# A hybrid decoder layer: when the second map's weight sums are loaded and added, and when the next block's inputs begin

## The chip, the cores and the metric

The kernel runs on one core of one Trainium2 chip. The metric is the device time of one execution in microseconds (us).

## The reference

One decoder layer on x of shape (1, 2048, 1024), float32, with a conditioning vector c:

```python
cond = jax.nn.silu(c)
mod = (cond @ w_ada + b_ada)[:, None, :]
sh1, sc1, g1, sh2, sc2, g2 = jnp.split(mod, 6, axis=-1)

h = x * (1.0 + sc1) + sh1
z = h @ w_in                                   # 1024 -> 2048
gate_b, gate_c, v_conv, v_pool = jnp.split(z, [512, 1024, 1536], axis=-1)
y_conv = gate_b * _short_conv(gate_c * v_conv, conv_w)
y_pool = _multiscale_pool(v_pool, w_pool, pool_scale)
mix = jnp.concatenate([y_conv, y_pool], axis=-1) @ w_out
x = _layer_norm(ALPHA * x + (1.0 + g1) * mix, ln1_g, ln1_b)

h = x * (1.0 + sc2) + sh2
f = jnp.square(jax.nn.relu(h @ w_mlp_in)) @ w_mlp_out   # 1024 -> 4096 -> 1024
x = _layer_norm(ALPHA * x + (1.0 + g2) * f, ln2_g, ln2_b)
```

## The kernel before

The 2048 tokens are worked through in two blocks (b) of 1024. Each block passes through the input projection (in_proj_0 or in_proj_1), the output projection (out_proj) and the **first map** (first_map: 1024 -> 4096 with the squared ReLU). The **second map** (down: 4096 -> 1024) then runs once, over both blocks. Every product of float32 matrices is made of three matmuls (mm3, L161 to L164) from a high part (ScalarE, L157) and a low part (VectorE, L158) of each operand; this making of two parts is called a split here.

The large products use schemes with fewer products and more additions. In the first map each of eight groups g (512 columns of the hidden layer) takes seven products instead of eight. The weights of a product come from sums of blocks of w1, made on VectorE as they are needed (block_weights, L585, in block 0) or read back from DRAM (w1sum, in block 1). The activations' seven operands ("11", "21", "22", "1", "2", "3", "4") are made once a block by back, of which "1" to "4" need parts that are read back from DRAM (hsave, L864 and L879). A group's results (c11, c12, c22, c21) are then summed by the list U_SUMS into 26 blocks that the second map reads (usum, stored from the POOL queue, L1080).

The second map takes 26 products over 4 x 4 x 2 blocks (PRODUCTS). Their weights are 8 raw blocks of w2 and 17 sums of them, each made once, in eight column halves g of 512 columns, by **sum_down** (L1145). It follows the list W_SUMS: an entry of two is a load of a block into a register (half of an "o" tile) through SP's queue (L1153), an entry of five an addition on VectorE (all additions have the helper's line, L167), and where its last number is not -1 the result is stored to DRAM (wsum, from the POOL queue, L1159). sum_down is a generator: it hands control back ahead of each addition.

What calls it is **beside**, which up (the first map of one group) calls between its products, four times in group 0 and seven times in each other group. In block 0 beside takes the next step of first_side: four steps that make the gate vector g2 from wada (ada, two loads and two products each), twelve steps of two sum_down entries each, between them four sums of the next block's inputs (sum_x), two of the input projection's weights (sum_weights), and then second_side, which goes on with sum_down, two additions a step. In block 1 beside takes second_side from the start.

At the start of a block, first_map runs the first products of groups 0 and 1 between the steps of back; five calls of beside fall into that part. After the last group of block 0, **prepare** (L698) loads and splits the next block's first weight and three of its seven inputs.

The "o" tiles are a pool of ten buffers of 128 x 1024. A group's four results, its spare tiles for sums, sum_down's two register tiles, the wada rows, sum_x and sum_weights, the parts that back reads from hsave, and out_proj's eight rows of x all come from it. The framework plans the order of each engine's and each queue's instructions when the kernel is built: the earlier in the program, the sooner, but an instruction whose buffer is not free stands back for later ones that can run. On the chip each engine and queue then runs in that order and waits on semaphores.

Of the kernel before, what the change touches and what calls it, by code (L numbers as in the profile page):

```python
# [11 lines left out]
ALU = mybir.AluOpType  # L12
# [6 lines left out]
NB = S // T  # L19
# [5 lines left out]
NC = FF // FC  # L25
# [7 lines left out]
SLOTS = 26  # L33
RAW_SLOT = (0, 4)
U_SUMS = (
# [4 lines left out]
)  # L40
W_SUMS = (
    (3, 6),
    (2, 7),
    (1, 3, 2, -1, 8),
    (0, 4),
    (2, 0, 3, -1, 9),
    (0, 2),
    (3, 0, 3, -1, 10),
    (3, 1, 0, -1, 11),
    (0, 0),  # L50
    (2, 2, 0, 1, 12),
    (2, 1, 0, -1, -1),
    (0, 1),
    (2, 2, 0, 1, 13),
    (2, 3, 0, 1, 14),
    (2, 3),
    (3, 3, 2, 1, 15),
    (3, 5),
    (2, 2, 3, -1, -1),
    (3, 7),  # L60
    (3, 0, 3, -1, 16),
    (3, 2, 3, -1, 17),
    (3, 4),
    (1, 1, 3, -1, 18),
    (0, 1, 0, 1, -1),
    (3, 0, 2, -1, 19),
    (3, 0),
    (0, 0, 3, -1, 20),
    (2, 0, 2, -1, 21),
    (3, 2),  # L70
    (2, 2, 3, 1, 22),
    (2, 5),
    (0, 0, 2, 1, 23),
    (1, 1, 2, 1, 24),
)
W_KEPT = 25
PRODUCTS = (
    (13, 2, 1, True, ((3, 0, 1), (3, 1, 1))),
    (2, 3, 1, True, ((0, 1, 1),)),
    (15, 11, 1, False, ((3, 1, -1),)),  # L80
    (5, 23, -1, False, ((2, 1, -1), (3, 1, 1))),
    (23, 8, 1, False, ((0, 0, 1),)),
    (19, 5, 1, False, ((1, 1, 1),)),
    (25, 4, -1, False, ((1, 0, 1),)),
    (4, 17, 1, True, ((2, 1, -1),)),
    (3, 21, 1, True, ((0, 0, -1), (1, 0, -1), (3, 0, -1))),
    (7, 19, 1, False, ((0, 1, -1),)),
    (0, 12, 1, False, ((1, 0, 1),)),
    (1, 22, -1, False, ((0, 0, -1), (2, 0, -1))),
    (6, 20, 1, False, ((1, 1, 1),)),  # L90
    (21, 7, -1, True, ((1, 1, -1),)),
    (8, 16, 1, False, ((2, 1, -1),)),
    (24, 18, 1, False, ((1, 0, -1),)),
    (10, 14, -1, False, ((2, 0, -1),)),
    (22, 9, 1, False, ((0, 0, -1),)),
    (9, 10, -1, False, ((3, 0, 1),)),
    (20, 24, 1, False, ((0, 1, -1),)),
    (14, 15, -1, False, ((3, 1, 1),)),
    (17, 13, -1, True, ((3, 0, 1),)),
    (11, 3, 1, True, ()),  # L100
    (18, 0, 1, False, ((2, 0, -1),)),
    (16, 1, 1, False, ((2, 1, 1),)),
    (12, 2, -1, True, ((2, 0, 1),)),
)

WARM = (5, 3, 1, 2, 2, 2)
# [13 lines left out]
def tile_hybrid_layer(ctx: ExitStack, tc: tile.TileContext, opening, xT, x, wada, win,  # L120
# [921 lines left out]
    def sum_out(g, tiles):  # L1042
        sum_blocks([gout[i % 2, i // 2 * 2 + g] for i in range(4)], wosum[g], tiles)

    def up(b, g, B, beside):
        X, Y, Z = {}, {}, {}
        order = (0, 1, 5, 4, 6, 7, 3) if g else (0, 1, 7, 4, 5, 6, 3)
        product = seven(summed_weights(w1[g], w1sum[g], order) if b or g < 2 else block_weights(w1[g], w1sum[g]), B)
# [78 lines left out]
        if g == 0:  # L1127
            yield
        else:
            product(5, Z, False)  # L1130
            join(c12, Z)
            beside()
# [11 lines left out]

    def sum_down():  # L1145
        for g in range(NC):
            tiles = [t_o() for _ in range(2)]
            regs = [r[:, hs] for r in tiles for hs in halves]
            for step in W_SUMS:
                if len(step) == 2:  # L1150
                    to, i = step
                    src = w2[i, g // 2] if i < 8 else wsum[i - 8, g // 2]
                    nc.sync.dma_start(regs[to], src[:, halves[g % 2]])  # L1153
                    continue
                yield
                to, x, y, sign, i = step
                tt(regs[to], regs[x], regs[y], ALU.add if sign > 0 else ALU.subtract)
                if i >= 0:
                    nc.gpsimd.dma_start(wsum[i - 8, g // 2][:, halves[g % 2]], regs[to])  # L1159

    def residual():
        ag, ab = row(t_o(D), rows[0]), row(t_o(D), rows[1])
# [10 lines left out]
                yield  # L1173


    def down(g2, close):
        F = close.F
        lo_, hi_ = halves
        banks = {}
# [89 lines left out]
        for k, (n, gp) in enumerate(stream):  # L1269
            if n == last:  # L1270
                break
            if k + 4 < len(stream):
                ready.append(operand(*stream[k + 4]))
            ops = ready.pop(0)
            _, _, _, new, reads = PRODUCTS[n]
            if gp == 0:
                if new:
                    banks[n % 2] = [t_ps() for _ in range(4)]
                if 3 <= n < 12:
                    next(later)  # L1280
# [89 lines left out]
    def first_side():  # L1370
        for n in range(0, 8, 2):
            ada(G2 + n, G2 + n + 2, nc.sync.dma_start, lambda: t_o(D))
            yield
        weights = sums_down
        for n in range(4):
            for _ in range(3):
                next(weights)
                next(weights)
                yield
            sum_x(n)  # L1380
            yield
        g2 = mk(sm, [P, D], F32, "bc", 1)
        row_by_dram(g2, mod[:, G2 : G2 + KD], 1)
        gate.append(g2)
        for p in halves:
            sum_weights(wins[0], winsum, t_o, which=[p])
            yield
        yield from second_side()

    def second_side():  # L1390
        for _ in sums_down:
            next(sums_down, None)
            yield

    gate = []
    sums_down = sum_down()

    def first_map(b, B, back):
        side = second_side() if b else first_side()
        rest = []  # L1400

        def beside():
            next(side, None)

        ups = [up(b, g, B, beside) for g in range(NC)]
        for g in range(2):
            next(ups[g])
            back(1 + g)
        for i in range(3, 7):
            next(ups[0])  # L1410
            back(i)
        for g in range(NC):
            for _ in ups[g]:
                pass

    ready = None
    for b in range(NB):
# [64 lines left out]
```

## Time and profile before

| | |
|---|---|
| median of 3 runs | 1974.24 us (1971.22 to 1982.32) |
| the profiled execution | 1976.97 us, its span 1975.1 us |
| TensorE busy | 1741.5 us, 88% of the span |
| VectorE busy | 1422.5 us, 72% |
| ScalarE busy | 839.7 us, 43% |
| POOL busy (it issues the stores) | 402.2 us, 20% |
| moved by DMA | 481.04 MB, 244 GB/s |
| granted TensorE clock, mean | 0.937 |

A row of the timeline has the start in us from the span's start, the duration in us, engine, source line, operation, what is written and read, how many were merged, and in brackets the idle time before it with what ended that. In a windows table each row is one stretch of the span with its length, then busy time and count for each engine, the granted clock as a share of full speed, the DMA engines' busy share and GB/s. SPq is SP's queue, which issues loads. Tiles are named without their numbers; o<-in_w is a load from a raw weight, in sum_down's case from w2.

### The profile page before, as it was taken

Reading aid. Unit: us, or ns where it says so; the run is one execution under the profiler, and the core shown is the slowest. Engines: PE = TensorE matmul, PEld = TensorE weight load, DVE = VectorE, ACT = ScalarE, POOL = GpSimd, SP = SyncE. Lnnn points to the kernel's source line nnn. Section 1 sums busy time; section 2 is a strip of 40 time slices with the busy share of each in tenths; the row PEclk is TensorE's granted clock in tenths of the full one; section 3 lists DMA queues with packets and bytes.
Section 4 is the critical chain, followed back from the end, with each engine's and each line's share of the span. In section 5 each row is a group of like instructions: output and inputs, shape, how many; then the busy total and the mean of one; then the engine's idle time right before and its main releaser. Section 6 shows DMA issues by size and latency. Waiting matters only on the chain.

```text
span 1975.1 us, 22593 instructions
## 1 busy us (share of the span) xinstructions
PE 1741.5 (88%) x7519; PEld 1422.8 (72%) x7519; DVE 1422.5 (72%) x2222; ACT 839.7 (43%) x1148; POOL 402.2 (20%) x767
## 2 busy tenths in 40 slices
PE   9999986218968875899998889789999999999998
PEld 8888865207756654778886667677788888888887
DVE  7987867327767676688967667667666487686998
ACT  6332463105533335434475433334554434353551
POOL 0223120214444343011010444344200000000000
PEclk9999997659988988999999898989999999999999
DMA  9989684437887778644754778767887688667782
GB/s 390 351 304 354 236 295 132 157 107 243 294 287 244 233 266 278 218 172 175 265 193 138 230 227 272 256 215 243 289 290 255 226 287 319 215 220 245 238 309 75
DMA packets 156357, 481.04 MB, mean 244 GB/s; under 512 B 22728, under 2 KB 23248, under 8 KB 156240
## 3 DMA queue, kind: packets, MB, share of 16 engines
q1 hardware_dynamic: 102112, 306.53, 45.8%
q0 software_dynamic: 54128, 173.07, 24.2%
q8 instruction: 59, 0.97, 0.2%
q14 instruction: 58, 0.48, 0.1%
HBM read 317.50 MB, written 162.01 MB: 243 GB/s over the span
## 4 chain that ended last, share of the span: by engine, by line
PE 41%; issue 11%; DMA 11%; DVE 6%; POOL 3%; ACT 1%; DVEq 0%; SPq 0%; POOLq 0%; ACTq 0%
PE ps L163 14%; PE ps L164 14%; PE ps L162 13%; DVE o L167 4%; DMA o<-in_w 4%; DMA wsum<-o 3%; POOL usum L1080 2%; DMA usum<-o 2%; POOL wsum L1159 1%; DVE w L158 1%; DMA o<-hsave 1%; DVE r L167 0%; DMA xsum<-o 0%; DMA r<-usum 0%; PE ps L841 0%
## 5 line engine op out<-in xcount | busy, mean ns | idle before, releaser
L162 PE MATMUL ps<-h,w 128*128 128x512 f32 x1312 | 530.3, 405 | 145.7 <-ACT h L157 104.1
L164 PE MATMUL ps<-h,w 128*128 128x512 f32 x1312 | 527.4, 403 | 64.9 <-DVE w L158 64.8
L163 PE MATMUL ps<-h,w 128*128 128x512 f32 x1312 | 526.6, 401 | 3.0 <-DVE h L158 2.9
L163 PE MATMUL ps<-h,h 128*128 128x512 f32 (+1 forms) x1064 | 412.4, 388 | 0.9 <-DVE h L158 0.9
L162 PE MATMUL ps<-h,h 128*128 128x512 f32 (+1 forms) x1064 | 412.6, 388 | 0.5 <-ACT h L157 0.5
L164 PE MATMUL ps<-h,h 128*128 128x512 f32 (+1 forms) x1064 | 412.4, 388 | 0.0
L162 PEld LDWEIGHTS ps<-h,w 128*128 128x128 f32 x1312 | 256.9, 196 | 208.2 <-ACT h L157 106.9
L167 DVE TENSOR_TENSOR o<-o,o 128x256 f32<-128x256 f32 (+2 forms) x570 | 272.6, 520 | 153.6 <-DMA o<-in_w 108.0
L164 PEld LDWEIGHTS ps<-h,w 128*128 128x128 f32 x1312 | 255.6, 195 | 128.1 <-DVE w L158 73.9
L163 PEld LDWEIGHTS ps<-h,w 128*128 128x128 f32 x1312 | 256.2, 195 | 60.3 <-DVE h L158 6.3
L1080 POOL DMA_DIRECT2D usum<-o x416 | 222.4, 541 | 237.3 <-DVE o L167 164.7
L157 ACT CAST w<-r 128x1024 fp32r<-128x1024 f32 x156 | 163.5, 1051 | 187.6 <-PE ps L163 174.2
L157 ACT CAST h<-r 128x1024 fp32r<-128x1024 f32 (+1 forms) x140 | 140.7, 1010 | 237.1 <-PE ps L163 109.6
L163 PEld LDWEIGHTS ps<-h,h 128*128 128x128 f32 x1064 | 199.8, 188 | 41.9 <-DVE h L158 1.3
L162 PEld LDWEIGHTS ps<-h,h 128*128 128x128 f32 x1064 | 199.8, 188 | 41.8 <-ACT h L157 0.9
L164 PEld LDWEIGHTS ps<-h,h 128*128 128x128 f32 x1064 | 199.8, 188 | 40.9
L158 DVE TENSOR_TENSOR w<-r,w 128x1024 fp32r<-128x1024 f32 x156 | 189.3, 1220 | 41.1 <-ACT w L157 40.9
L158 DVE TENSOR_TENSOR h<-r,h 128x1024 fp32r<-128x1024 f32 (+1 forms) x140 | 162.6, 1167 | 62.5 <-ACT h L157 62.4
L167 DVE TENSOR_TENSOR o<-o 128x256 f32<-128x256 f32 (+1 forms) x224 | 118.9, 535 | 117.7 <-DMA o<-in_w 52.8
L1159 POOL DMA_DIRECT2D wsum<-o x136 | 73.5, 541 | 347.0 <-DVE o L167 335.7
L1067 ACT ACTIVATE o<-o 128x1024 f32<-128x1024 f32 x48 | 50.9, 1060 | 203.7 <-DVE o L167 203.6
L158 DVE TENSOR_TENSOR h<-w,h 128x1024 fp32r<-128x1024 f32 x104 | 126.7, 1219 | 1.6 <-ACT h L157 1.3
(163 smaller groups left out, 1457.5 us busy)
## 6 DMA issues: line engine op xcount, KB each, us to landing
usum<-o POOLq DMA_DIRECT2D x416, 128.0 KB, 4.5
r<-usum SPq DMA_DIRECT2D x104, 512.0 KB, 5.1
wsum<-o POOLq DMA_DIRECT2D x136, 256.0 KB, 3.5
w<-wsum SPq DMA_DIRECT2D x68, 512.0 KB, 5.3
o<-in_w SPq DMA_DIRECT2D x112, 256.0 KB, 4.1
r<-in_w SPq DMA_DIRECT2D x54, 512.0 KB, 5.2
r<-w1sum SPq DMA_DIRECT2D x40, 512.0 KB, 4.5
w<-in_w SPq DMA_DIRECT2D x36, 512.0 KB, 5.9
```

What stands on the lines that cost most here:

```text
L157: high = nc.scalar.copy(hi, src)
L158: return high.ins, nc.vector.tensor_tensor(lo, src, hi.bitcast(F32), op=ALU.subtract).ins
L162: nc.tensor.matmul(ps, whi, xhi, start=first, stop=False, skip_group_check=goes_on)
L163: nc.tensor.matmul(ps, whi, xlo, start=False, stop=False, skip_group_check=goes_on)
L164: nc.tensor.matmul(ps, wlo, xhi, start=False, stop=last, skip_group_check=goes_on)
L167: return nc.vector.tensor_tensor(out_, a, b_, op=op)
L1067: nc.scalar.activation(r, r, AF.Relu)
L1080: nc.gpsimd.dma_start(usum[slot, g // 2, :, b, g % 2, :], z)
L1159: nc.gpsimd.dma_start(wsum[i - 8, g // 2][:, halves[g % 2]], regs[to])
```

## The change

It has four parts.

1. W_SUMS is rewritten as 11 steps. Each step first makes its additions (two, none in the first step) and then issues the loads of the next one, into registers that no addition of this step touches. sum_down holds three tiles (six registers) where it held two (four), and hands control back once a step. A column half has 12 loads where it had 13, and 20 additions and 17 stores as before.
2. U_SUMS and PRODUCTS are replaced by another form of the same scheme: 33 additions a group as before, two spare tiles where there were three, 26 products as before, of which eight have a negated operand where nine had.
3. beside does nothing until a flag (open_) is set, after the part in which back makes the operands. first_side takes four sum_down steps ahead of each sum_x, and block 1's beside takes sum_down directly. What is left of sum_down at the end is taken by down, one step a unit of work (next(side, None)), where before it was run through ahead of down.
4. prepare is called by turn, from the last group of block 0, ahead of its sixth product, where before it was called after the whole first map.

The diff without the tables U_SUMS and PRODUCTS, and with the old W_SUMS cut:

```diff
 W_SUMS = (
-    (3, 6),
-    (2, 7),
-    (1, 3, 2, -1, 8),
-    (0, 4),
-    (2, 0, 3, -1, 9),
...
+    ((), ((0, 4), (1, 6), (3, 2))),
+    (((2, 0, 1, -1, 8), (4, 3, 1, -1, 9)), ((5, 7),)),
+    (((1, 1, 5, -1, 10), (3, 1, 3, -1, 11)), ((4, 1), (0, 0))),
+    (((5, 4, 5, -1, 12), (2, 2, 0, 1, 13)), ()),
+    (((0, 0, 4, -1, -1), (4, 3, 4, 1, 14)), ((2, 3),)),
+    (((3, 3, 2, 1, 15), (5, 5, 2, -1, -1)), ((4, 5),)),
+    (((5, 5, 4, 1, 16), (2, 1, 0, -1, 17)), ((3, 4),)),
+    (((1, 1, 3, -1, 18), (4, 1, 4, 1, 19)), ()),
+    (((2, 1, 0, -1, 20), (3, 0, 4, -1, 21)), ((5, 3),)),
+    (((4, 4, 5, -1, -1), (0, 0, 4, -1, 22)), ((1, 2), (2, 1))),
+    (((1, 0, 1, -1, 23), (4, 4, 2, 1, 24)), ()),
 )
...
-    def up(b, g, B, beside):
+    def up(b, g, B, beside, turn):
...
         else:
+            if g == NC - 1:
+                turn()
             product(5, Z, False)
             join(c12, Z)
             beside()
...
     def sum_down():
         for g in range(NC):
-            tiles = [t_o() for _ in range(2)]
+            tiles = [t_o() for _ in range(3)]
             regs = [r[:, hs] for r in tiles for hs in halves]
-            for step in W_SUMS:
-                if len(step) == 2:
-                    to, i = step
-                    src = w2[i, g // 2] if i < 8 else wsum[i - 8, g // 2]
-                    nc.sync.dma_start(regs[to], src[:, halves[g % 2]])
-                    continue
+            cs = halves[g % 2]
+            for adds, loads in W_SUMS:
+                for to, x, y, sign, i in adds:
+                    tt(regs[to], regs[x], regs[y], ALU.add if sign > 0 else ALU.subtract)
+                    if i >= 0:
+                        nc.gpsimd.dma_start(wsum[i - 8, g // 2][:, cs], regs[to])
+                for to, i in loads:
+                    nc.sync.dma_start(regs[to], (w2[i, g // 2] if i < 8 else wsum[i - 8, g // 2])[:, cs])
                 yield
-                to, x, y, sign, i = step
-                tt(regs[to], regs[x], regs[y], ALU.add if sign > 0 else ALU.subtract)
-                if i >= 0:
-                    nc.gpsimd.dma_start(wsum[i - 8, g // 2][:, halves[g % 2]], regs[to])
...
-    def down(g2, close):
+    def down(g2, close, side):
...
             if n == last:
                 break
+            next(side, None)
             if k + 4 < len(stream):
...
-        weights = sums_down
         for n in range(4):
-            for _ in range(3):
-                next(weights)
-                next(weights)
+            for _ in range(4):
+                next(sums_down)
                 yield
             sum_x(n)
             yield
...
-        yield from second_side()
-
-    def second_side():
         for _ in sums_down:
-            next(sums_down, None)
             yield
...
     def first_map(b, B, back):
-        side = second_side() if b else first_side()
-        rest = []
+        side = sums_down if b else first_side()
+        open_ = []
 
         def beside():
-            next(side, None)
-
-        ups = [up(b, g, B, beside) for g in range(NC)]
+            if open_:
+                next(side, None)
+
+        def turn():
+            if b + 1 < NB:
+                ready.append(prepare())
+
+        ups = [up(b, g, B, beside, turn) for g in range(NC)]
         for g in range(2):
             next(ups[g])
             back(1 + g)
         for i in range(3, 7):
             next(ups[0])
             back(i)
+        open_.append(True)
         for g in range(NC):
             for _ in ups[g]:
                 pass
 
-    ready = None
+    ready = []
     for b in range(NB):
-        B, back = out_proj(b, in_proj_1(*ready) if b else in_proj_0())
+        B, back = out_proj(b, in_proj_1(*ready[0]) if b else in_proj_0())
         first_map(b, B, back)
-        if b == 0:
-            ready = prepare()
-    for _ in sums_down:
-        pass
-    close = Close()
-    down(gate[0], close)
+    down(gate[0], Close(), sums_down)
```

More of the change, by code (lines that the diff above doesn't have):

```diff
@@ L35 @@
 U_SUMS = (
[4 rows of a table removed]
[4 rows of a table added]
 )
 W_SUMS = (
-    (3, 6),
-    (2, 7),
-    (1, 3, 2, -1, 8),
-    (0, 4),
-    (2, 0, 3, -1, 9),
[L47 to L74, printed above, removed]
[11 rows of a table added]
 )
@@ L77 @@
 PRODUCTS = (
[L78 to L103, printed above, removed]
+    (11, 2, 1, True, ((3, 0, 1), (3, 1, 1))),
+    (1, 3, 1, True, ((0, 1, 1),)),
+    (17, 11, 1, False, ((3, 1, -1),)),
+    (5, 21, 1, False, ((2, 1, -1), (3, 1, 1))),
+    (24, 10, 1, False, ((0, 0, 1),)),
+    (21, 5, 1, False, ((1, 1, 1),)),
+    (23, 4, -1, False, ((1, 0, 1),)),
+    (4, 16, -1, True, ((2, 1, -1),)),
+    (3, 22, 1, True, ((0, 0, 1), (1, 0, 1), (3, 0, 1))),
+    (6, 24, 1, False, ((0, 1, -1),)),
+    (0, 13, -1, False, ((1, 0, -1),)),
+    (2, 23, 1, False, ((0, 0, -1), (2, 0, -1))),
+    (8, 20, -1, False, ((1, 1, -1),)),
+    (20, 7, -1, True, ((1, 1, -1),)),
+    (9, 12, -1, False, ((2, 1, 1),)),
+    (25, 18, 1, False, ((1, 0, -1),)),
+    (12, 14, 1, False, ((2, 0, 1),)),
+    (22, 8, 1, False, ((0, 0, -1),)),
+    (7, 9, 1, False, ((3, 0, -1),)),
+    (19, 19, 1, False, ((0, 1, -1),)),
+    (13, 15, 1, False, ((3, 1, -1),)),
+    (15, 17, -1, True, ((3, 0, 1),)),
+    (18, 3, 1, True, ()),
+    (14, 0, 1, False, ((2, 0, -1),)),
+    (10, 1, 1, False, ((2, 1, 1),)),
+    (16, 2, -1, True, ((2, 0, 1),)),
 )
```

8 rows, old and new, of the table U_SUMS are left out of this document.

## The prediction

> **What bounds the kernel now.** I read the page's parts 1 and 2 first, then TensorE's stages, then its longest idle times, and last the queues that stood in the way.
>
> ```profile
> span 1975.1 us, 22593 instructions
> PE 1741.5 (88%) x7519; PEld 1422.8 (72%) x7519; DVE 1422.5 (72%) x2222; ACT 839.7 (43%) x1148; POOL 402.2 (20%) x767
> PE   9999986218968875899998889789999999999998
> PEclk9999997659988988999999898989999999999999
> ```
>
> TensorE is the bound nearly everywhere. Counting slices from 0, it falls away in 6 to 15 (block 0's first map) and a little in 21 to 26 (block 1's), and there the granted clock falls too. The stages, in one table by windows: block 0's first map up to the first matmul after its long stall, the rest of that map, block 1's two projections, block 1's first map in the same two parts, and the second map.
>
> ```profile
> core 0: us, PE busy (x) PEld busy (x) DVE busy (x) ACT busy (x) POOL busy (x), PEclk, DMA share, GB/s
> 275.30:438.90 163.60, 60.80 (x249) 48.27 (x247) 73.29 (x110) 35.81 (x45) 23.06 (x43) 0.67 0.45 154
> 438.90:795.00 356.10, 281.90 (x1134) 223.92 (x1135) 254.56 (x450) 151.04 (x182) 151.38 (x283) 0.89 0.78 261
> 795.00:1040.40 245.40, 242.59 (x1084) 199.95 (x1084) 194.40 (x271) 121.39 (x194) 25.67 (x45) 0.99 0.58 205
> 1040.40:1112.00 71.60, 58.76 (x231) 46.07 (x232) 46.97 (x63) 32.78 (x39) 11.89 (x23) 0.88 0.46 146
> 1112.00:1410.00 298.00, 267.80 (x1121) 217.02 (x1121) 201.24 (x387) 124.89 (x148) 124.66 (x233) 0.94 0.75 243
> 1410.00:1975.10 565.10, 556.24 (x2475) 460.99 (x2473) 419.39 (x523) 252.58 (x348) 10.14 (x19) 1.00 0.71 248
> ```
>
> The last row gives the price of a matmul when nothing is in its way: 556.24 / 2475 = 0.2247 us. At that price the second row's 1134 matmuls need 254.8 us of its 356.1, so 101 us are lost there, idle and slow clock together; the fifth row's 1121 need 251.9 of 298.0, so 46 are lost. Rows one and four are the same program part in the two blocks (transposes, the making of seven operands, the first products), yet one takes 163.6 us and the other 71.6.
>
> TensorE's longest idle times, from its timeline (the bracket is the idle time before the instruction, and what ended it):
>
> ```profile
> 289.01 0.48 PE L841 MATMUL ps<-ident,o 128*128 128x128 f32 x1 [6.49 <-DVE o L167]
> 329.79 0.79 PE L162 MATMUL ps<-h,w 128*128 128x512 f32 x1 [14.95 <-ACT h L157]
> 438.93 0.79 PE L162 MATMUL ps<-h,w 128*128 128x512 f32 x1 [78.85 <-ACT h L157]
> 794.72 0.79 PE L164 MATMUL ps<-h,w 128*128 128x512 f32 x1 [17.75 <-DVE w L158]
> ```
>
> The 78.85 us is a hole in which VectorE adds weights and the other engines stand. Its cause is read from SP's, ScalarE's and VectorE's timelines in turn:
>
> ```profile
> 357.54 4.62 SPq L1153 DMA_DIRECT2D o<-in_w  x3
> 367.29 61.46 SPq L1153 DMA_DIRECT2D o<-in_w  x10
> 432.37 5.09 SPq L879 DMA_DIRECT2D o<-hsave  x2
> 437.83 1.04 ACT L157 CAST h<-o 128x1024 fp32r<-128x1024 f32 x1 [76.90 <-DVE o L167]
> 412.40 0.69 DVE L167 TENSOR_TENSOR o<-o,o 128x512 f32<-128x512 f32 x1 [5.31 <-DMA o<-in_w]
> 436.57 1.23 DVE L167 TENSOR_TENSOR o<-o,o 128x1024 f32<-128x1024 f32 x1 [4.23 <-DMA o<-hsave]
> ```
>
> Operand "4" needs the two hsave loads (L879), and these stand on SP behind 13 loads of L1153: exactly one full set of W_SUMS. Each add of 0.69 us waits up to some 5 us for a load that could not be issued until the register was free. I infer why the set stands first: hsave needs two of the ten "o" buffers, and two of those were held by sum_down until its set was through.
>
> Outside the hole the same adds hold VectorE up all through both first maps (its waits, first 438.9 to 795, then 1112 to 1410, last the w2 loads of the whole profile; columns: sum in us, times, longest):
>
> ```profile
> DVE o L167 <- DMA o<-in_w: 49.9, 23, 4.8
> DVE o L167 <- DMA wsum<-o: 12.0, 4, 6.4
> ...
> DVE o L167 <- DMA o<-in_w: 55.6, 25, 5.4
> DVE o L167 <- DMA wsum<-o: 17.5, 11, 4.6
> ...
> DVE o L167 <- DMA o<-in_w: 160.8, 65, 5.4
> ```
>
> That is 61.9 us in the one and 73.1 in the other, on an engine that runs in order, so the weight splits and the additions out of PSUM queue behind.
>
> **The change part by part.** The sum is made against the profiled execution's 1976.97 us, 2.7 above the median of the three runs shown.
>
> *No sums before the operands exist (open_).* Five calls of beside per block now do nothing. In the order of the changed kernel's instructions the L879 hsave loads stand on SP ahead of all wada loads and all w2 loads, and their adds on VectorE ahead of the first wada product. So the hole's cause is gone. What is late next is what the fourth row shows, where no sum stood in the way before either: 71.6 us for 231 instructions. With 249 it is 71.6 + 18 x 0.2247 = 75.6, against 163.6: 88 us gained. The eight wada products that filled this part move into the next one:
>
> ```profile
> 284.64 1.23 DVE L278 SCALAR_TENSOR_TENSOR o<-o,o 128x1024 f32<-128x1024 f32 x1 [4.95 <-DMA o<-in_wada]
> L1153 SPq DMA_DIRECT2D o<-in_w x44: 327/328/762, 492.0 to 788.6; - x44
> DMA to landing us min/median/max: 2.6/4.5/8.7
> L1159 POOL DMA_DIRECT2D wsum<-o x136 | 73.5, 541 | 347.0 <-DVE o L167 335.7
> ```
>
> They are 8 x 1.23 = 9.8 us of VectorE. There it is busy 254.56 of 356.1 us, so between 0 and 9.8 show; I take 4. Net 84.
>
> *Two additions a step, loads a step ahead, three tiles instead of two.* Per column half 12 loads instead of 13 (eight fewer in all, 0.33 us each on SP: 2.6 us, hidden, as SP mostly waits); the 20 additions (0.69) and 17 stores (0.54 on POOL) stay. A step now ends with the loads for the next, so a load has one product of 24 matmuls, 24 x 0.2247 = 5.4 us, to land. The landing row (of L1153, 438.9 to 795) has a median of 4.5 and a longest of 8.7, so most waits vanish and some stay. Leaving out the 17.75 us gap, which is the next part's, 101.3 - 17.8 = 83.5 us were lost. Bounds: nothing comes back, if the split waits have other causes; or all of it. I take six tenths, 50 us, nearer the upper end because 61.9 us of VectorE's waits are these loads and stores. In block 1 the additions run on, in the changed order, to the last two groups, which had none. There the bounds are -10 and 46; I take 20.
>
> *Next block's inputs begin sooner (turn).* prepare is moved ahead of the last group's products 5 and 6 and of the sums after them on VectorE; its loads now stand among the last w2 loads on SP, and it has none on POOL. Before, ScalarE and VectorE made the first weight so:
>
> ```profile
> 773.80 1.04 ACT L157 CAST w<-r 128x1024 fp32r<-128x1024 f32 x1 [1.56 <-DMA r<-in_wins]
> 793.45 1.22 DVE L158 TENSOR_TENSOR w<-r,w 128x1024 fp32r<-128x1024 f32 x1
> ```
>
> The second half of that split came 19 us after the first, behind the last group's sums, and cost TensorE the 17.75 us. In the changed order it stands ahead of product 5's own weight split, with five adds of the weights (0.69) and two input subtractions (1.22) between them. So the gap goes, and product 5 may wait instead: 5 x 0.69 + 2 x 1.22 = 5.9 us, of which I let 4 show. Bounds 0 and 17.75; I take 14.
>
> *Other tables.* 33 additions a group in U_SUMS before and after, with two spare tiles where there were three; four fewer negated operands, whose instructions cost what the plain ones do. The second map has no loss to give: zero. The sums that end in it are the last two additions, 1.4 us, under a VectorE 419 of 565 us busy; if that cover failed, 1.4 us.
>
> Sum: 84 + 50 + 20 + 14 = 168. 1976.97 - 168 = 1809, less 2.7 for the median: 1806 us.
>
> **The rivals.**
>
> *All of the stalls go.* If VectorE's load waits are the cause of nearly everything lost, 84 + 75 + 40 + 16 = 215 come back: 1759. For it: 61.9 and 73.1 us of waits against 83 and 46 lost. Against it: VectorE stays 72% busy there and so has its own work to wait for. 18%.
>
> *The clock comes back whole.* After a long gap the matmuls are slow for a while: the one at 331.70, 1.9 us behind the gap of 14.95, took 0.63 us, and the line's mean is 403 ns.
>
> ```profile
> 331.70 0.63 PE L164 MATMUL ps<-h,w 128*128 128x512 f32 x1
> L164 PE MATMUL ps<-h,w 128*128 128x512 f32 x1312 | 527.4, 403 | 64.9 <-DVE w L158 64.8
> ```
>
> The clock's share of what is lost is 281.90 - 254.8 = 27 us in the second stage and 267.80 - 251.9 = 16 in the fifth. My sum takes six and four tenths of it back, 23. If gaps that are only shortened leave the clock alone, all 43 come back: 20 more, 1786. The Trainium skill (TensorE: Matmul & The Clock Gate, "Part 1: The HAM clock gate") says that the clock halves only after an idle window of about 3.4 us and recovers after as much work. The gap of 14.95 agrees; no row above shows a short gap by itself. 8%.
>
> *The DMA engines become the bound.* The second stage has 0.78 of 356.1 us, 278 us of transfer, which does not shrink with the gaps. Loads issued early then land late. If half of the 50 and nothing of block 1's 20 come back, 84 + 25 + 0 + 5 = 114: 1860. The Trainium skill (DMA: Bandwidth & Descriptors, "Issuing engines are not separate DMA queues") says that all queues share the same 16 engines; the stage table cannot tell that from a slow queue. 15%.
>
> *The change doesn't do what it says: the hole comes back in another place,* where a set of sums again holds "o" buffers that the path needs. Then 50 + 20 + 14 remain and the 84 don't: 1890. Against it: in the changed order each set of the first map ends before out_proj, which takes eight of ten. 4%.
>
> *Slower: three register tiles starve the pool of ten.* Six for a group's results and sums and three for sum_down leave one. The next group's second result then waits for a store to land.
>
> ```profile
> ACT o L1055 <- DMA usum<-o: 15.3, 3, 8.2
> ```
>
> It has happened three times, 8.2 at the longest. If it hit both results of each of 14 later groups at that length, 14 x 2 x 8.2 = 230 us would go, against 168 gained: 2036. It decides from 168 / 28 = 6 us each. Against it: 4 + 3 + 2 buffers before are as many as 4 + 2 + 3. 4%.
>
> **How the numbers follow.** The forecast keeps 50%. The range 1740 to 1870 takes in the first three rivals, with a little beyond the first since the bounds (88, 83.5, 46, 17.75) add up to 235, which is 1739. Half a percent, 10 us, is about what a measurement tells from no change (the three runs lie 11 apart). Faster by that: the forecast and the first four rivals, 0.95; within it 0.01, left for a gain that other waits eat up; slower 0.04.
>
> **What would show it.** Right: no TensorE gap over 20 us; the hsave loads of L879 ahead of every w2 load; the first map's first part near 76 us in both blocks; VectorE's waits on w2 loads below 50 us in the whole profile, from 160; the second map still 565. Wrong: a stretch of ten w2 loads in a row with TensorE idle, or a DMA share over 0.9 with VectorE still waiting for loads.

## The result and the profile after

The changed kernel takes 1848.5 us (median of 4 runs, 1846.85 to 1848.79) against 1975.22 (1971.22 to 1982.32) for the kernel before, run beside it: a ratio of 0.9353, 95% interval 0.9325 to 0.9381. That is 127 us faster, inside the predicted range, and 42 us short of the predicted 1806. Its profiled execution took 1848.79 us, its span 1846.8.

The page's parts 1 and 2 of the changed kernel:

```profile
span 1846.8 us, 22581 instructions
PE 1726.5 (93%) x7519; PEld 1415.0 (77%) x7519; DVE 1420.4 (77%) x2222; ACT 840.1 (45%) x1148; POOL 402.7 (22%) x767
PE   9999998777959889999988999899999999999998
PEclk9999998888989999999989999999999999999999
```

The work is the same (7519 matmuls, 2222 VectorE instructions). TensorE's dips in slices 6 to 15 have become shallower (5 tenths at the lowest, in slice 11, where slice 8 had 1), and the clock no longer falls below 8 tenths. The same six stages by windows, cut at the same matmuls as before (columns as in the prediction):

```profile
275.00:347.20 72.20, 57.90 (x248) 45.91 (x247) 49.90 (x70) 35.41 (x45) 13.90 (x26) 0.92 0.50 168
347.20:682.50 335.30, 275.57 (x1134) 221.65 (x1135) 260.31 (x462) 150.49 (x181) 147.88 (x277) 0.89 0.85 291
682.50:930.20 247.70, 242.45 (x1085) 200.28 (x1083) 197.31 (x279) 123.18 (x196) 29.48 (x52) 0.99 0.57 202
930.20:1000.30 70.10, 57.50 (x232) 45.22 (x233) 46.88 (x63) 32.49 (x39) 11.83 (x23) 0.90 0.44 143
1000.30:1281.70 281.40, 263.36 (x1121) 213.87 (x1120) 213.46 (x407) 124.48 (x148) 133.98 (x250) 0.98 0.86 281
1281.70:1846.80 565.10, 556.14 (x2474) 461.16 (x2472) 419.42 (x523) 252.80 (x348) 10.29 (x20) 1.00 0.70 249
```

Stage by stage, before minus after: 163.6 - 72.2 = 91.4 (predicted 88); 356.1 - 335.3 = 20.8 (predicted 50 - 4 + 14 = 60); 245.4 - 247.7 = -2.3; 71.6 - 70.1 = 1.5; 298.0 - 281.4 = 16.6 (predicted 20); 0. The sum is 128, and nearly the whole miss lies in the rest of block 0's first map. (The time is nearer to the 1860 of the rival with the DMA engines than to 1806; the runs below tell whether that rival was at work.)

SP's queue after (timeline), where the hole was: the hsave loads for operand "4" (L857 now) stand ahead of the wada and w2 loads.

```profile
340.15 3.08 SPq L857 DMA_DIRECT2D o<-hsave  x2
343.33 0.88 SPq L566 DMA_DIRECT2D r<-in_w  x2
349.46 25.49 SPq L265 DMA_DIRECT2D o<-in_wada  x8
375.05 1.33 SPq L1136 DMA_DIRECT2D o<-in_w  x3
```

What is left in the rest of block 0: its three largest TensorE gaps, the ScalarE instructions that stood ahead of the casts behind the first and the third (timelines of TensorE and of ScalarE), then VectorE's waits, in the whole profile and (last two rows) in this stage:

```profile
387.44 0.79 PE L140 MATMUL ps<-h,w 128*128 128x512 f32 x1 [9.57 <-ACT w L135]
452.88 0.80 PE L142 MATMUL ps<-h,w 128*128 128x512 f32 x1 [10.04 <-DVE w L136]
552.77 0.79 PE L140 MATMUL ps<-h,w 128*128 128x512 f32 x1 [18.65 <-ACT w L135]
```

```profile
384.28 1.08 ACT L1118 ACTIVATE o<-ps 128x512 f32<-128x512 f32 x2 [8.78 <-DMA usum<-o]
539.24 1.08 ACT L1118 ACTIVATE o<-ps 128x512 f32<-128x512 f32 x2 [12.30 <-DMA winsum<-o]
```

```profile
DVE o L145 <- DMA o<-in_w: 62.5, 34, 6.2
DVE o L145 <- DMA wsum<-o: 9.7, 4, 6.3
...
DVE o L145 <- DMA o<-in_w: 25.0, 9, 6.2
DVE o L145 <- DMA wsum<-o: 3.4, 3, 1.6
```

VectorE's waits on w2 loads fell from 160.8 us to 62.5 (the prediction's sign was below 50), in this stage with the stores from 61.9 to 28.4. ScalarE stands at c21 (L1118) for an "o" buffer whose store has not landed, with the weight casts queued behind it. This is not new: the kernel before waited 11.1 us for a store of winsum at the same place. Behind the third gap ScalarE has two more waits, 3.00 us for a store of usum and 4.16 us for an addition on VectorE, before the cast.

### The profile page after: what moved, and what is told of

The parts are those of the page before. It is cut to its first block, busy times and chain, and to the rows that moved or that the text cites. A ratio compares the mean times of both kernels' runs of the same rounds, so it can differ in the third digit from the quotient of the medians.

```text
span 1846.8 us, 22581 instructions
## 1 busy us (share of the span) xinstructions
PE 1726.5 (93%) x7519; PEld 1415.0 (77%) x7519; DVE 1420.4 (77%) x2222; ACT 840.1 (45%) x1148; POOL 402.7 (22%) x767
## 5 line engine op out<-in xcount | busy, mean ns | idle before, releaser
L140 PE MATMUL ps<-h,w 128*128 128x512 f32 x1312 | 523.9, 400 | 58.8 <-ACT w L135 34.5
L142 PE MATMUL ps<-h,w 128*128 128x512 f32 x1312 | 522.7, 399 | 38.2 <-DVE w L136 38.2
L141 PE MATMUL ps<-h,w 128*128 128x512 f32 x1312 | 521.9, 398 | 8.1 <-DVE h L136 8.0
L140 PEld LDWEIGHTS ps<-h,w 128*128 128x128 f32 x1312 | 252.5, 193 | 118.5 <-ACT w L135 37.3
L142 PEld LDWEIGHTS ps<-h,w 128*128 128x128 f32 x1312 | 253.1, 193 | 97.6 <-DVE w L136 44.6
L145 DVE TENSOR_TENSOR o<-o,o 128x256 f32<-128x256 f32 (+2 forms) x554 | 266.0, 524 | 70.5 <-DMA o<-in_w 23.9
L141 PEld LDWEIGHTS ps<-h,w 128*128 128x128 f32 x1312 | 253.1, 193 | 64.3 <-DVE h L136 11.1
L135 ACT CAST h<-r 128x1024 fp32r<-128x1024 f32 (+1 forms) x144 | 144.8, 1011 | 240.4 <-PE ps L141 131.1
L136 DVE TENSOR_TENSOR h<-r,h 128x1024 fp32r<-128x1024 f32 (+1 forms) x144 | 167.5, 1170 | 86.0 <-ACT h L135 85.8
L145 DVE TENSOR_TENSOR o<-o 128x256 f32<-128x256 f32 (+1 forms) x240 | 124.9, 528 | 69.2 <-DMA o<-in_w 38.6
L145 DVE TENSOR_TENSOR o<-o,ps 128x512 f32<-128x512 f32 x172 | 114.1, 683 | 22.9 <-PE ps L142 19.5
```

Source lines behind the costliest of these rows:

```text
L135: high = nc.scalar.copy(hi, src)
L136: return high.ins, nc.vector.tensor_tensor(lo, src, hi.bitcast(F32), op=ALU.subtract).ins
L140: nc.tensor.matmul(ps, whi, xhi, start=first, stop=False, skip_group_check=goes_on)
L141: nc.tensor.matmul(ps, whi, xlo, start=False, stop=False, skip_group_check=goes_on)
L142: nc.tensor.matmul(ps, wlo, xhi, start=False, stop=last, skip_group_check=goes_on)
L145: return nc.vector.tensor_tensor(out_, a, b_, op=op)
```

## The experiments

Line numbers differ from kernel to kernel. The stages are cut at the same matmuls in all, and come from one profiled execution of each. The ratio compares a kernel with the kernel before of its own group of runs (medians 1970.63 to 1978.89 us). Differences in us in the text are those of the times, where no ratio is named; by the ratios they would be up to 6 us larger or smaller.

| kernel | us | ratio to before, 95% | block 0 first part | its rest | block 1 rest |
|---|---|---|---|---|---|
| before | 1975.22 | 1 | 163.6 | 356.1 | 298.0 |
| changed | 1848.5 | 0.9353 (0.9325 to 0.9381) | 72.2 | 335.3 | 281.4 |
| no_flag | 1874.56 | 0.9485 (0.9458 to 0.9513) | 97.1 | 330.0 | 271.3 |
| no_lead | 1851.5 | 0.9376 (0.9357 to 0.9396) | 72.4 | 345.5 | 279.9 |
| prep_after | 1851.58 | 0.9372 (0.9354 to 0.939) | 71.7 | 341.1 | 277.8 |
| sums_late | 1890.48 | 0.9576 (0.9551 to 0.96) | 72.0 | 287.5 | 368.2 |
| no_adds | 1805.38 | 0.9157 (0.9137 to 0.9177) | 72.4 | 321.8 | 254.5 |
| two_tiles | 1918.49 | 0.9737 (0.971 to 0.9764) | 70.9 | 375.8 | 315.5 |
| two_tiles_no_flag | 1927.72 | 0.9775 (0.975 to 0.9801) | 94.5 | 359.4 | 309.8 |
| pool_adds | 1900.55 | 0.9642 (0.9612 to 0.9673) | 72.3 | 365.9 | 304.0 |
| w5 | 1888.38 | 0.9541 (0.951 to 0.9571) | 80.3 | 353.7 | 298.2 |
| w5_o11 | 1870.42 | 0.9454 (0.9428 to 0.948) | 71.7 | 346.4 | 299.8 |
| gate_late | 1873.76 | 0.9465 (0.9432 to 0.9497) | 71.8 | 343.4 | 288.1 |
| before_new_u | 1906.52 | 0.9672 (0.9652 to 0.9692) | 96.3 | 366.4 | 288.8 |

**no_flag.**

```diff
-        open_ = []
+        open_ = [True]
```

> The changed kernel (1848.5 us) with beside working from the start of each block again (open_ set at once). The first map's first part in block 0 took 163.6 us before and 72.2 after. Theory of the prediction: the hole came from sums taken before the operands exist, so without the flag it comes back: first part over 130 us, total over 1900 us. Rival: the flag is only half of it. In this kernel's order only four w2 loads stand on SP ahead of the hsave loads of operand 4, where a full set of 13 stood before, because three tiles and loads a step ahead let a set go on differently. Then the first part takes some 72 + 8 x 1.23 (the wada products are back in it) + a few load waits = 85 to 95 us, the rest of block 0's map gets shorter by about as much, and the total lies within 10 us of 1848.5.

The first part grew by 25 us, not by 91, and block 1's by as much. Both stages by windows:

```profile
275.20:372.30 97.10, 59.32 (x248) 46.92 (x246) 60.75 (x91) 35.77 (x45) 14.99 (x28) 0.80 0.59 197
945.80:1041.00 95.20, 60.14 (x232) 46.98 (x233) 59.98 (x83) 32.87 (x39) 21.02 (x40) 0.78 0.56 184
```

Against 72.2 and 70.1 with the flag. The rests got 5 and 10 us shorter, and the total 26 longer. The rival came nearer for block 0's first part, the total lies between the two. So the flag is worth about 26 us, and most of the hole is gone without it. In block 1 it keeps out a loss that the kernel before did not have. There the first part took 71.6 us without any flag, and 71.0 in two_tiles_no_flag (below); with three tiles and loads a step ahead, SP's queue has ten w2 loads ahead of block 1's first hsave loads:

```profile
945.81 11.39 SPq L1136 DMA_DIRECT2D o<-in_w  x4
...
960.58 0.33 SPq L1136 DMA_DIRECT2D o<-in_w  x1
...
968.04 1.62 SPq L1136 DMA_DIRECT2D o<-in_w  x2
...
975.91 5.34 SPq L1136 DMA_DIRECT2D o<-in_w  x3
986.37 1.27 SPq L842 DMA_DIRECT2D o<-hsave  x2
```

**no_lead.** Each step's loads go ahead of its own additions.

```diff
+            due = ()
             for adds, loads in W_SUMS:
+                for to, i in due:
+                    nc.sync.dma_start(regs[to], ...)
+                due = loads
...
-                for to, i in loads:
-                    nc.sync.dma_start(regs[to], ...)
```

> The changed kernel with each step's loads issued ahead of its own additions instead of at the end of the step before; tables, three tiles, additions, stores and flag as they are. It prices the lead alone, for which the prediction took 50 us in block 0 and 20 in block 1 (with the change of form). Theory A (VectorE's waits for w2 loads are what the lead takes away, and they reach TensorE): the waits on w2 loads go from 62.5 us back to 130 to 160, and the total grows by 35 to 70 us, about 1885 to 1920. Theory B (the lead takes VectorE's waits away, but most of them were off the path; block 0's rest is held by the other work of first_side): the waits grow just as much, but the total by under 20 us.

3 us, within the intervals of no change. The waits on w2 loads hardly moved (62.5 in the changed kernel); those on the stores of sums grew from 9.7 to 22.1 us:

```profile
DVE o L145 <- DMA o<-in_w: 61.0, 30, 8.0
DVE o L145 <- DMA wsum<-o: 22.1, 9, 5.4
```

Neither theory held, since both expected the waits on w2 loads to double. Block 0's rest grew by 10.2 us, and the projections behind it and block 1 gave most of that back. The framework's plan seems to put a load where its register comes free, wherever the program has it, so that the lead lies in the free registers (the next two runs).

**prep_after.** The call of turn stands after the whole first map.

```diff
-            if g == NC - 1:
-                turn()
             product(5, Z, False)
...
+        turn()
```

> The changed kernel with prepare called after the whole first map of block 0 again, as before. It prices the earlier inputs alone. Theory of the prediction: the gap of 17.75 us before the projections of block 1 comes back, and 14 us net are lost: 1862.5 us. Rival 1: the gap was the tail of the sums of the last group, which now run otherwise, so under 5 us are lost: below 1853.5. Rival 2: earlier inputs cost as much on the last group as they save (ties within 3 us).

3.1 us longer, within the intervals; not the predicted 14. The gap of 17.75 us did not come back as one. TensorE's timeline has two in its place:

```profile
680.98 0.80 PE L140 MATMUL ps<-h,w 128*128 128x512 f32 x1 [7.03 <-ACT w L135]
...
687.49 0.79 PE L142 MATMUL ps<-h,w 128*128 128x512 f32 x1 [4.44 <-DVE w L136]
```

Block 0's rest grew by 5.8 us, and the other stages gave part of it back. Rival 1 held; rival 2, a tie within 3 us, can't be told from it.

**two_tiles and two_tiles_no_flag.** sum_down in its old form (its code as before), with a list of 32 entries for four registers, worked out for the new sums; the second also sets the flag at once. These show what the lead lives on, and whether the hole comes back.

```diff
-            tiles = [t_o() for _ in range(3)]
+            tiles = [t_o() for _ in range(2)]
...
```

> The changed kernel with sum_down as before in form: two tiles (four registers), each load directly ahead of the addition that needs it, two additions a call; same sums, again 20 additions, 12 loads (one of them of a stored sum). The flag and the tables of the first map stay. Moving the loads alone had cost 3 us. Theory R (what lets a load run ahead is a free register, so the third tile is the lead): VectorE's waits on w2 loads go from 62.5 us to over 120, block 0's rest from 335 to 350 or more, block 1's from 281 to 295 or more, total 1875 to 1910 us. Rival P (the ten buffers are what is short in block 0; one buffer more free for results and for first_side is worth as much as the lead): the total stays within 10 us of 1848.5 or falls, with the longest waits of ScalarE on stores (12.3 us) gone.

> The kernel two_tiles with beside working from the start of each block again. With three tiles and no flag the first part of block 0's first map took 97.1 us where it took 163.6 before and 72.2 with the flag. Theory of the prediction (two register tiles, held until the set is through, keep the hsave loads back): the hole comes back in this kernel, first part over 140 us, total 45 us or more over two_tiles. Rival S (the third spare tile of the old first map's sums was what left no buffer for hsave; with two spares there is room): the first part is 85 to 105 us, as with three tiles, and the total within 30 us of two_tiles. In this kernel's order three w2 loads stand ahead of the first hsave load of operand 4 and one more ahead of the second, which speaks for S.

VectorE's waits in the whole of two_tiles:

```profile
DVE o L166 <- DMA o<-in_w: 132.1, 55, 7.1
DVE o L166 <- DMA wsum<-o: 22.5, 11, 5.9
```

Theory R held in its direction: without the third tile the waits double, and 70 us are lost, 40.5 in block 0's rest and 34.1 in block 1's; the total passed its upper end. The 70 us are an upper bound for the tile, since the order of this list is my own: two_tiles_no_flag is 21 us slower than before_new_u (below), which keeps the old list. With two tiles the flag is worth 9 us (1927.72 - 1918.49), with three 26. Without the flag the first part took 94.5 us. So two register tiles and a missing flag together do not bring the hole of 163.6 back, and rival S's times held.

**before_new_u.** The kernel before, with the changed kernel's U_SUMS and nothing else. Its second map still reads the stored blocks by the old numbers, so it computes something else; the work is the same.

```diff
 U_SUMS = (
-    ((1, 5, -1, 1, 16), (0, 1, 1, 2, 1), (16, 0, 1, 3, 19)),
+    ((0, 1, 1, 1, 16), (1, 5, -1, 2, 1), (17, 0, 1, 3, 19)),
...
```

> The kernel before with one thing changed: its list U_SUMS is that of the changed kernel (33 additions a group, two spare tiles instead of three). The list W_SUMS and PRODUCTS stay, so the numbers of the second map are others; the work is the same. Two register tiles, no flag, loads just ahead of their additions, prepare after the first map. Theory S (the hole stood there because the third spare tile left no buffer for the hsave loads until a whole set of sums was through): three w2 loads, not 13, stand on SP ahead of the hsave loads of operand 4 here, so the first part of block 0's first map takes 90 to 105 us instead of 163.6. The set that ran in the hole then costs its price in the rest (10 calls at about 1.3 us), so the total is 45 to 65 us below 1974, 1909 to 1929 us. Theory of the prediction (sums taken too early by two register tiles held until the set ends; the flag was needed): the hole stays, first part over 140 us, the total within 15 us of 1974.

Its first part and the rest of block 0 by windows, then SP's queue:

```profile
275.10:371.40 96.30, 59.29 (x249) 46.94 (x247) 60.95 (x93) 35.74 (x45) 15.04 (x28) 0.80 0.58 196
371.40:737.80 366.40, 282.74 (x1135) 225.15 (x1136) 267.12 (x468) 152.49 (x184) 160.13 (x298) 0.87 0.81 275
```

```profile
351.42 9.12 SPq L1153 DMA_DIRECT2D o<-in_w  x3
362.04 0.33 SPq L879 DMA_DIRECT2D o<-hsave  x1
...
371.22 0.33 SPq L879 DMA_DIRECT2D o<-hsave  x1
```

Three w2 loads ahead of the first hsave load, where 13 stood before: the list alone takes 67 us out of the first part and gives 10 back in the rest; in block 1's rest it brings 9.2. In all it brings 65 us, half of the change's 127. It was the edit that the prediction costed at zero. The old list takes its third spare tile in its second row, which group 0 runs just ahead of operand "4", and the new one never takes a third. That this tile is what matters was not separated from the order of the additions: no run changed the one without the other. Nor does the old list make a hole wherever it runs: in block 1 of the kernel before, with no flag either, the hsave loads stood ahead of the w2 loads (71.6 us). And no run has the old list with the flag, so whether the flag alone would have removed the hole stays open.

**sums_late and no_adds.** The first takes no step of sum_down in block 0 and two a call in block 1; the second leaves the 160 additions out, stores loaded blocks in place of sums, and keeps loads, stores and tiles.

```diff
-                next(sums_down)
                 yield
...
+    def second_side():
         for _ in sums_down:
+            next(sums_down, None)
             yield
...
-        side = sums_down if b else first_side()
+        side = second_side() if b else first_side()
```

```diff
-                    tt(regs[to], regs[x], regs[y], ALU.add if sign > 0 else ALU.subtract)
                     if i >= 0:
-                        nc.gpsimd.dma_start(wsum[i - 8, g // 2][:, cs], regs[to])
+                        nc.gpsimd.dma_start(wsum[i - 8, g // 2][:, cs], regs[got])
                 for to, i in loads:
+                    got = to
...
```

> The changed kernel with no step of sum_down in block 0; block 1's beside takes two steps a call instead. It tells what holds the rest of block 0's first map, which took 335.3 us with 1134 matmuls (254.8 us at 0.2247 each, so 80.5 us are lost). Theory B (the waits behind ada, sum_x and the sums of the projection's weights, whose loads are used at once and whose tiles come from the same ten buffers): with sum_down's loads, additions and three tiles all gone, at least half of the loss stays: the stage over 295 us. Theory A (sum_down's own loads and additions hold it): the stage falls to 255 to 275 us. Block 1's rest, 281.4 us with 48 steps, takes 88: longer by 10 us if the lead covers the loads, by 40 or more if they come late at a DMA share that would pass 0.95.

> The changed kernel without sum_down's 160 additions: loads (256 KB each), stores, the three tiles and the steps stay, what is stored is a loaded block (so the second map's weights are others). Without any of sum_down, block 0's rest had fallen from 335.3 to 287.5 us; this tells which part of it did that. Theory V (VectorE runs in order; an addition that waits for its load, 25.0 us there, and the 0.69 us of each hold up the weight splits): the stage falls to 285 to 305 us and block 1's rest from 281.4 to 258 to 268; the total to 1775 to 1810 us. Rival D (DMA engines busy 0.85 of the stage, and buffers that stay held until stores land): the stage stays over 320 us, block 1's over 275, and the total over 1825 us.

The two rests by windows, first of sums_late, then of no_adds:

```profile
347.50:635.00 287.50, 266.24 (x1135) 217.07 (x1135) 223.38 (x399) 153.64 (x185) 118.71 (x222) 0.95 0.76 253
951.80:1320.00 368.20, 280.18 (x1121) 223.56 (x1120) 258.78 (x479) 121.96 (x145) 168.82 (x315) 0.87 0.87 294
```

```profile
347.60:669.40 321.80, 276.26 (x1135) 222.16 (x1136) 225.35 (x404) 152.42 (x184) 153.17 (x286) 0.91 0.91 318
983.20:1237.70 254.50, 254.15 (x1121) 210.12 (x1120) 167.10 (x327) 125.93 (x148) 134.37 (x250) 1.00 0.95 312
```

The two blocks differ. In **block 1** the additions with their waits are nearly the whole loss: without them 254.5 us, below theory V's range, where 1121 matmuls at full speed need 251.9. There the DMA engines are busy 0.95 of the stage at 312 GB/s, and TensorE loses 2.6 us: rival D, as it was put, is out there. The run takes away an addition's own time (80 x 0.69 = 55 us in this stage) and its wait for a load (36.5 us in the changed kernel) together, so it can't say whether loads that landed late were behind the loss. In **block 0** rival D's bound was met (321.8, over 320). Taken away in this order, the loss of 80.5 us (335.3 - 254.8) falls into 13.5 us that go with the additions (335.3 - 321.8), 34.3 that go with sum_down's loads, stores and tiles (321.8 - 287.5), and 32.7 that stay with no sum_down at all. For sums_late both thresholds were missed, 287.5 lying between them; the 40 steps put into block 1 cost it 86.8 us, 2.2 each, where the 38 taken from block 0 had cost 1.3.

**pool_adds.**

```diff
-                    tt(regs[to], regs[x], regs[y], ALU.add if sign > 0 else ALU.subtract)
+                    nc.gpsimd.tensor_tensor(regs[to], regs[x], regs[y], op=...)
```

> The changed kernel with sum_down's 160 additions on POOL instead of VectorE, nothing else changed. No row shows what POOL takes for one; VectorE takes 0.69 us, POOL is busy 22% of the span. Theory V (VectorE's order is what the additions disturb): block 0's rest falls to 290 to 315 us, block 1's to 260 to 270, total 1790 to 1825 us. Rival (POOL also issues the stores of the first map's sums, which then queue behind additions that wait for loads, so buffers come free later; or the two engines slow each other): the stage stays at 335 us or grows, total 1850 to 1930 us, and ScalarE's and VectorE's waits on usum stores grow.

The rival's times held, 52 us slower. POOL's additions from the groups, then the weight splits on VectorE, in pool_adds and in the changed kernel (duration in ns min/median/max):

```profile
L1132 POOL TENSOR_TENSOR o<-o,o 128x512 f32<-128x512 f32 x96 | 145.4, 1517 | 19.1 <-DMA o<-in_w 13.1 <-DMA wsum<-o 4.3
L136 DVE TENSOR_TENSOR w<-r,w x156: 1205/1221/5743, 47.6 to 1295.0; 128x1024 fp32r<-128x1024 f32 x156
```

```profile
L136 DVE TENSOR_TENSOR w<-r,w x156: 1205/1221/1232, 47.1 to 1256.7; 128x1024 fp32r<-128x1024 f32 x156
```

POOL takes 1.52 us where VectorE takes 0.69, and a split of VectorE took up to 5.74 us (at 503.45, across three additions on POOL), where none takes over 1.23 without POOL's additions. The Trainium skill (SBUF — State Buffer, "Who interferes with whom") says that a VectorE instruction with two SBUF inputs contends with a GpSimd instruction that reads SBUF; the trace agrees, 5.74 against 1.23 us. Of the rival's two reasons only this one is seen: ScalarE's and VectorE's waits on usum stores did not grow (22.6 us in the changed kernel, 22.1 here).

**w5, w5_o11 and gate_late.** An eleventh "o" buffer, paid with a sixth w buffer, and its control; and the gate vector's wada work moved to block 1 (its lines go from first_side into a second_side that block 1 takes).

```diff
-        return mk(big, [P, w], dt, "o", 10)
+        return mk(big, [P, w], dt, "o", 11)
...
-        return mk(big, [P, T], dt, "w", 6)
+        return mk(big, [P, T], dt, "w", 5)
```

> The changed kernel with five w buffers instead of six: the control for the kernel w5_o11, which needs that space. Weights are split into pairs of w buffers, so five give two pairs and one more half. Both theories expect it to be slower than 1848.5, by 5 to 40 us; only its difference to w5_o11 tells something.

> The control w5 with eleven o buffers instead of ten. Theory P (in block 0's rest the ten buffers are what is short: there ScalarE waited 12.3 us for a store of the projection's weights and 8.8, 4.9 and 3.0 us for stores of the first map's sums before it could write an o tile, 29 us in all, and TensorE's gaps of 9.6 and 18.7 us stand behind the first two): block 0's rest is 12 to 30 us shorter than the control's, those waits fall below 12 us, and the total is 10 to 35 us below the control. Rival L (loads that come late and VectorE's order hold the stage, a buffer more only lets SP load sooner): less than 6 us.

> The changed kernel with the four ada steps of the gate vector g2 (eight wada tiles from the ten buffers, eight products of 1.23 us) at the start of block 1's beside calls instead of block 0's; the sums of the second map then begin four calls sooner in block 0. Theory P: the gap of 9.6 us at 387 us, where the ada tiles held buffers, goes, and nothing as large comes in block 1, whose calls have no sum_x and no sums of the projection's weights beside them: total 5 to 15 us less, 1833 to 1843 us. Rival: the work costs in block 1 what it cost in block 0, or sums of the second map fill the place at 1.3 us a step: within 4 us of 1848.5.

The rest of block 0 in w5 and in w5_o11:

```profile
355.40:709.10 353.70, 283.23 (x1136) 224.31 (x1134) 262.42 (x467) 153.60 (x184) 150.44 (x281) 0.90 0.83 277
```

```profile
346.80:693.20 346.40, 282.36 (x1135) 223.62 (x1134) 263.20 (x469) 153.39 (x184) 149.94 (x280) 0.91 0.83 281
```

The buffer is worth 7.3 us there, between the theories' bounds, and 18 in all, 8.6 of it in the first part. ScalarE's waits for stores fell in this stage from 31.3 us to 15.3, its longest, on the store of winsum, only from 12.5 to 11.2. gate_late missed in sign: 25 us slower (22 by the ratio), with 8.1 us more in the rest of block 0 though the wada tiles were gone from it, and 12.2 more in block 1's two parts. The gap of 9.57 us at 387 did not go but moved: one of 11.99 stands at 401.83, again behind a wait of ScalarE for a usum store. Four more steps of sum_down took the wada work's place in block 0, so the run shows that moving this work gains nothing, not that its tiles cost nothing. No kernel here with the layer's whole work beats the changed one.

## Why the prediction was right, and where it was wrong

- **The hole (88 us; 91.4 measured).** The size held, and so did the sign that was named: hsave loads ahead of every w2 load, 72.2 and 70.1 us in the two blocks. The reason given did not. "So the hole's cause is gone" was credited to open_; the form of U_SUMS, under *Other tables* at zero, takes 67 out by itself, and behind it the flag is worth 25 us there. The step that failed is the inference that "two of those were held by sum_down until its set was through", as the whole reason: with two tiles and no flag, but the new list, the hole stays away. That the flag would have done it with the old list, no run shows.
- **The shares.** Three kernels make a chain from before to changed: before_new_u (0.9672), no_flag (0.9485), changed (0.9353). In this order U_SUMS brings 65 us, the new W_SUMS with its third tile, PRODUCTS and the earlier inputs 37, and the flag 26. The prediction gave them 0, 84 (50 + 20 + 14) and 84. Another order could share it out otherwise, since the flag and U_SUMS act on the same hole. But that the total came near with such shares is in part luck.
- **Two additions a step, three tiles, in block 0 (50 us).** This is the mis-sized term. The stage gave 20.8, where 60 were forecast with the other two terms; the predicted 4 for the wada work is near the 5.3 us by which no_flag's rest is shorter. The step was "because 61.9 us of VectorE's waits are these loads and stores". Those waits did fall, to 28.4 (25.0 and 3.4), though the loads landed later than in the row that the prediction used (median 5.0 us and longest 10.3, where it had 4.5 and 8.7). But without any additions only 13.5 of the stage's 80.5 us come back. A wait on VectorE counts by what stands behind it, and in this stage TensorE mostly waited for something else too. What the remaining 34.3 and 32.7 us are stays open between late loads and buffers held by stores: one buffer more gave 7.3, and moving the wada work gave none.
- **The same in block 1 (20 us; 16.6, and 1.5 in the first part).** Here the step held as to the loss: no_adds shows that VectorE's additions and their waits make it. The gain is less its own: before_new_u, with two tiles and the old W_SUMS, already has 288.8 us, so 9.2 of the 16.6 came with U_SUMS, and 7.4 are left for the third tile and the other parts (34 by two_tiles is an upper bound for the tile). The place of the loads in the program bought nothing (no_lead, 279.9). That 16.6 lies near 20 is in part luck.
- **The inputs that begin sooner (14 us).** Locally as forecast: the gap of 17.75 went. But undoing it alone costs 3 us, 5.8 in the stage, so most of that gap had gone with the other parts. That it came from the last group's sums, which now run otherwise, fits this and is not shown.
- **The rivals.** Not all stalls went. The DMA engines do not hold TensorE directly in block 1 (0.95 busy in no_adds, 2.6 us lost); late loads behind the additions there, and the engines in block 0, are not ruled out. The clock gave back 6.3 and 4.4 us (281.90 - 275.57 and 267.80 - 263.36), less than the 16 and 6 in the sum. The pool of ten did not starve: TensorE's longest gap is 18.65 us.

## What to carry to other kernels

When a scheduler plans the order around a shared pool of buffers, a table of additions that takes other tiles can move a critical load further than the flag written for it: look at who holds the buffers when the load is due, and test one edit at a time, the ones costed at nothing too. Here a load's lead came with free registers more than with the line where the load is written. Before counting an engine's waits as gain, take the waiting instructions out in one stage: in one block here that gave nearly everything back, in the other a sixth.

## What the runs showed of the hardware

The matmuls went to the slow rate after short gaps, and not by their length alone. TensorE's timelines, first of the kernel before, then of the changed kernel (two gaps), each with what follows:

```profile
546.65 0.64 PE L164 MATMUL ps<-h,w 128*128 128x512 f32 x1 [1.80 <-DVE w L158]
547.09 0.63 PE L162 MATMUL ps<-h,w 128*128 128x512 f32 x1
...
625.68 0.64 PE L142 MATMUL ps<-h,w 128*128 128x512 f32 x1 [2.64 <-DVE w L136]
626.11 0.63 PE L140 MATMUL ps<-h,w 128*128 128x512 f32 x1
...
1111.72 0.50 PE L142 MATMUL ps<-h,w 128*128 128x512 f32 x1 [3.03 <-DVE w L136]
1112.05 0.40 PE L140 MATMUL ps<-h,w 128*128 128x512 f32 x1
```

Ahead of all three gaps the matmuls took 0.39 us. After 1.80 and 2.64 us idle they ran at the slow rate (0.63 us); after 3.03 us they did not (0.40). The profile models the ends of matmuls, but from start to start the three are 2.18, 3.03 and 3.42 us, in the same order. The Trainium skill (TensorE: Matmul & The Clock Gate, "Part 1: The HAM clock gate") speaks of an idle window of about 3.4 us that runs freely; the first two rows are shorter than that, and the measurement decides. Several such short gaps are left in the rest of block 0, which may be why the clock gave back less than forecast; no run took them away alone.
